# Forming the second phase's weights beside the phase change instead of two blocks earlier

## The chip, the cores and the metric

The kernel runs on one core of one Trainium2 chip. The metric is the device time of one launch in microseconds (us); lower is better. A core has a matrix engine (TensorE, PE in the profile; its weight loads are listed as PEld), a vector engine (DVE), a scalar engine (ACT), GpSimd (POOL) and the sync engine (SP). Each runs its own queue of instructions in order. Transfers between device memory (DRAM) and on-chip memory (SBUF) are issued here by the SP, ACT and POOL queues; matrix products go to eight banks of PSUM, from which DVE or ACT must move them ("evict").

## The reference, cut to what matters

With one layer only the pooling mixer runs. x is 4096 x 1024, the model width 1024.

```python
normed = rms_norm(h, norm_w[i])
u, gate = jnp.split(h @ in_w, 2, axis=-1)        # in_w: 1024 x 2048, h is normed here
pooled = trailing means of u over 2, 4, 8, 16 rows (one window per 256 columns) - u
mixed  = einsum(pooled, group_w) + group_b       # per group of 256 columns
y = mixed * scale * silu(gate)
out = rms_norm(x + y @ out_w, final_norm_w)
```

All is float32.

## The kernel before, in words

**Folding and transposing.** The group map commutes with the pooling over rows, so the kernel folds `group_w` into the first half of `in_w` once, at the start (`fold`, L284). It keeps activations transposed, channels on the 128 partitions, and so works on 512 x 512 quarters of each 1024 x 1024 product.

**Products.** Each 1024 x 1024 x 1024 block product is made of seven half-size products P1 to P7 (a Strassen-Winograd scheme) instead of eight. For both operands this needs sums and differences of quarters: with quarters 11, 12, 21 and 22 of the weights, `combine` (L219) forms S = 22 - 12 for P7, T = 11 + S for P6, 22 - T for P5 and 21 - T for P4; P1, P2 and P3 use 11, 21 and 22 as they are. Order in the kernel: P1, P2, P6, P7, P5, P4, P3 (`ORDER_IN`).

**Splits.** For float32 accuracy each operand is split in two: a rounded high part (an ACT copy, L151) and the rest (a DVE subtraction, L145). `split` (L153) does both; `split_scaled` (L215) also multiplies rows by a column of scales. TensorE then runs three matmuls per tile, high x high, high x low, low x high (`mm3`, L457, L460). One product of the first two phases is 48 matmuls of 128x512.

**Phases and steps.** `steps` (L774) lists the work. Phase "a" makes columns 0 to 511 of both halves of the input projection (value path and gate), phase "b" columns 512 to 1023, each for four blocks of 1024 rows: 4 x 7 products a phase. Phase "o", the output projection with residual and final norm, has eight blocks of 512 rows with seven products of half the length. The loop at L995 runs step n: it loads ahead (three steps, L976), forms combinations, splits the operand of the next step, runs the product and evicts it (`run`, L808). The seven weight operands of a phase lie in `w[P1]` to `w[P7]`, in two tiles each (halves of the contraction, h = 0 and 1), and stay for all four blocks.

**Row statistics.** The first norm's row factors of the next block are computed during the current one: squares on ACT (L320), five small DVE instructions (`stats`, `rsqrt`), a 2 KB store to `rd` (L336) and a load that spreads it over all partitions (L363). `normalize` (L365, DVE at L148) multiplies the x tiles by it. The first half's factors are stored at step P5, the second's at P3; the second's are used by `normalize_a2` (L434) at P1 of the next block, from which S and T of the activations, and the splits, follow.

**Weights of phase b.** In blocks 1 and 2 of phase a, after product P5, `make_wb(h)` (L239) loads two pieces of `in_w` (L199) and two of the folded weights `wvd` (L243, L244), scales rows on ACT (L213), stores 11 and 21 to DRAM scratch `wbd` (L233, L234), combines on DVE (L142, L145) and stores the other five (L236). In the last block of phase a, right after product Pi has run, `load_w` (L257) loads both tiles of `wbd[i]` (L260) and splits them into `w[i]`, whose old content is no longer needed. Phase o's weights go the same way one phase later (`make_wo`, `wod`).

**Buffers and order.** Tiles come from two pools of 4 KB a partition, `st` (11) and `vt` (8), taken and given back in turn (`Slots`); a transfer into a tile waits for all that used it before. A scheduler places the instructions of each engine's queue from program order and priorities; `tc.issue_after(x)` keeps what is recorded under it behind x. Four tiles `ops` hold split activation operands; a step uses two.

Of the kernel before, what the change touches and what calls it, by code (L numbers as in the profile page):

```python
# [10 lines left out]
F32 = mybir.dt.float32  # L11
F32R = mybir.dt.float32r
AF = mybir.ActivationFunctionType
ALU = mybir.AluOpType

P = 128
D = 1024
S = 4096
H = 512
TB = 1024  # L20
NB = S // TB
# [9 lines left out]
P1, P2, P3, P4, P5, P6, P7 = range(1, 8)  # L31
ORDER_IN = (P1, P2, P6, P7, P5, P4, P3)
# [28 lines left out]
def kernel(  # L61
# [32 lines left out]
    nc = tc.nc  # L94
# [5 lines left out]
    dram = ctx.enter_context(tc.tile_pool(name="dram", bufs=1, space=bass.MemoryType.DRAM))  # L100
# [3 lines left out]
    def new_w(i):  # L104
        return [
            mem.tile([P, 2, 2, H], F32R, tag=f"w{i}_{h}", name=f"w{i}_{h}") for h in range(2)
        ]

    w = {i: new_w(i) for i in (P1, P2, P6, P7)}
# [18 lines left out]
    def take(pattern="p (a b) -> p a b", pool=None, **sizes):  # L128
        sizes = sizes or {"a": 2}
        if pool is None:  # L130
            spare = len(vt.free) > keep[0] or not st.free
            pool = vt if spare and vt.age() < st.age() else st
        return pool.take(lambda t: t[:, 0:D].rearrange(pattern, **sizes))
# [4 lines left out]
    def give(ap):  # L138
        next(p for p in (st, vt, early, early5) if id(ap) in p.used).give(ap)
# [4 lines left out]
    def sub(dst, a, b):  # L144
        nc.vector.tensor_tensor(out=dst, in0=a, in1=b, op=ALU.subtract)  # L145
# [4 lines left out]
    def copy(dst, src, func=AF.Copy):  # L150
        return nc.scalar.activation(dst, src, func)  # L151

    def split(dst, src):  # L153

        copy(dst[:, 0], src)
        sub(dst[:, 1], src, dst[:, 0].bitcast(F32))

    colt = const.tile([P, 24], F32, name="colt")
    norm_c = [colt[:, k : k + 1] for k in range(NK)]
    bias_c = [colt[:, 8 + k : 9 + k] for k in range(NK)]  # L160
# [2 lines left out]
    tails = const.tile([P, 2, 2, HIST], F32, name="tails")  # L163

    wvd = [dram.tile([P, 2, H], F32, name=f"wvd{k}") for k in range(4)]
    wbd = {
        i: [dram.tile([P, 2, H], F32, name=f"wbd{i}_{h}") for h in range(2)]
        for i in range(P1, P7 + 1)
    }
    wod = {  # L170
        i: [dram.tile([P, 2, H], F32, name=f"wod{i}_{h}") for h in range(2)]
        for i in range(P1, P7 + 1)
# [24 lines left out]
    def load_rows(mat, k, c):  # L197
        u = take()
        nc.sync.dma_start(  # L199
            out=u, in_=mat[k * P : (k + 2) * P, c : c + H].rearrange("(t p) c -> p t c", p=P)  # L200
        )
        return u
# [8 lines left out]
    def scale_rows(u, cs):  # L211
        for j in range(2):
            nc.scalar.activation(u[:, j], u[:, j], AF.Copy, scale=cs[j])  # L213

    def split_scaled(dst, u, cs):  # L215
        for j in range(2):
            copy_scaled(dst[:, :, j], u[:, j], cs[j])
# [10 lines left out]
    def pair(cs, h, kh):  # L228
        k = 4 * kh + 2 * h
        return cs[k : k + 2]  # L230

    def store_weights(dst, h, b11, b21, b12, b22):
        nc.sync.dma_start(out=dst[P1][h], in_=b11)  # L233
        nc.sync.dma_start(out=dst[P2][h], in_=b21)  # L234
        for i, u in combine(b11, b21, b12, b22).items():
            nc.sync.dma_start(out=dst[i][h], in_=u)  # L236
            give(u)

    def make_wb(h):  # L239
        g0 = load_rows(in_w, 2 * h, D + H)  # L240
        g1 = load_rows(in_w, 4 + 2 * h, D + H)
        v0, v1 = take(), take()
        nc.sync.dma_start(out=v0, in_=wvd[h])  # L243
        nc.sync.dma_start(out=v1, in_=wvd[2 + h])  # L244
        scale_rows(g0, pair(norm_c, h, 0))
        scale_rows(g1, pair(norm_c, h, 1))
        store_weights(wbd, h, g0, g1, v0, v1)

    def make_wo(h):
        us = {}  # L250
        for n in range(2):
            for kh in range(2):
                us[kh, n] = load_rows(out_w, 4 * kh + 2 * h, n * H)
                scale_rows(us[kh, n], pair(scale_c, h, kh))
        store_weights(wod, h, us[0, 0], us[1, 0], us[0, 1], us[1, 1])

    def load_w(src, i):  # L257
        for h in range(2):
            u = take()
            nc.sync.dma_start(out=u, in_=src[i][h])  # L260
            split(w[i][h], u)
            give(u)
# [296 lines left out]
    ev, evicted = {}, [None]  # L559
# [248 lines left out]
    def run(n, between=None):  # L808
        kind, b, i = steps[n]
        sets = sets_of(kind, b)  # L810
        if kind == "o":
            product_out(i, split_up.pop(n), sets, n == len(steps) - 1)
            evict_o(b, i, sets)
        else:
            product_in(i, split_up.pop(n), sets, i == P1, between)
            evict_in(b, 0 if kind == "a" else 1, i, sets)
# [30 lines left out]
    gw, ru, g0 = [None] * 2, {}, []  # L847
# [14 lines left out]
    v0, v1 = [None] * 2, [None] * 2  # L862
# [23 lines left out]
    g1 = [load_rows(in_w, 4 + 2 * h, D) for h in range(2)]  # L886
# [108 lines left out]
    for n in range(2, len(steps)):  # L995
        kind, b, i = steps[n]
        ahead = kind == "a" and b + 1 < NB
        keep[0] = 5 if kind == "b" and b == NB - 1 else 3
        advance("load", n, load, load_reach)
        if ahead:  # L1000
            rows, squares = row_plan(b)
            for half, rs in scales.items():
                store_rs(b + 1, half, rs)
                load_rstd(b + 1, half)
            scales.clear()
            for j in squares.get(i, ()):
                with tc.issue_after(evicted[0]):
                    square_row(b + 1, j // 4, j % 4)
                if j % 4 == 3:
                    scales[j // 4] = stats(b + 1, j // 4)  # L1010
            for j in rows.get(i, ()):
                load_row(b + 1, j // 4, j % 4, early if b == 0 and i == P6 else None)
        if kind == "a" and b > 0 and i == P1:
            normalize_a2(b)
        if n > 2:
            form(n + 2)
        advance("split", n, split_step, split_reach)
        if n == 2:
            form_s4(0)
            form(n + 2)  # L1020
        if kind == "a" and b == 0:
            rest_of_first(n)
        pool_due(n)
        run(n)
        if kind in ("a", "b"):
            pool_later(n)
            if kind == "a":
                pool_due(n)
            if b == NB - 1:
                load_w(wbd if kind == "a" else wod, i)  # L1030
            if i == P5:
                if kind == "a" and b in (1, 2):
                    make_wb(b - 1)
                elif kind == "b" and b in (1, 2):
                    make_wo(b - 1)
            if kind == "b" and b == NB - 1 and i == P3:
                f = take("p (a b) -> p a b", a=2)
                nc.sync.dma_start(
                    out=f.rearrange("p a b -> p (a b)"), in_=final_w.partition_broadcast(P)
                )  # L1040
                fw.append(f)
# [52 lines left out]
```

## Time and profile before

| what | us |
|---|---|
| median of three runs (971.11 to 971.44) | 971.4 |
| the profiled execution | 973.14 |
| its span, first to last instruction | 971.0 |
| PE busy | 951.5 |
| DVE busy | 745.6 |
| ACT busy | 452.2 |
| first product step of phase a starts | 39.74 |
| phase b starts | 353.62 |
| phase o starts | 658.26 |
| last product step starts | 957.46 |
| mean granted TensorE clock | 0.997 of full |

A row of busy times by stretch reads: stretch, its length, then busy us (and instructions) of PE, PEld, DVE, ACT and POOL, the granted clock, the DMA engines' busy share and GB/s. A row of the chain of waits reads: start, length, what the kernel's end hung on in that time; "DMA a<-b" is the time of a transfer. A row of DMA issues reads: tiles, issuing queue, count, size, median us from issue to landing.

### The profile page before, as it was taken

The numbers are of one execution on the slowest core, as the hardware profiler recorded it, in microseconds if no ns is written. First come the engines' busy times: TensorE is split into PE (matmuls) and PEld (weight loads), VectorE is DVE, ScalarE is ACT, GpSimd is POOL, SyncE is SP. The second block draws the span as 40 slices with busy tenths as digits, with TensorE's granted clock in tenths as the row PEclk, the third lists the DMA queues.
The fourth block names the chain that finished last, engine by engine and source line by source line (L and its number), as shares of the span: only waits on it lengthen the run. The fifth ranks groups of instructions, "written<-read, shape, count | busy, mean of one in ns | idle before, by whom it ended". The sixth has DMA issues, their size and how long they took to land.

```text
span 971.0 us, 11079 instructions
## 1 busy us (share of the span) xinstructions
PE 951.5 (98%) x4190; PEld 786.4 (81%) x4190; DVE 745.6 (77%) x907; ACT 452.2 (47%) x679; POOL 6.7 (1%) x16
## 2 busy tenths in 40 slices
PE   8899999989999999999999999999999999999996
PEld 7778888878877888888888888888888888888885
DVE  5696993886899794497598499599978677677675
ACT  4759438337545554345444435553424324324233
POOL 0100000000000000000000000000000000000000
PEclk9999999999999999999999999999999999999998
DMA  9964865977977624115714714646646446356022
GB/s 340 411 271 141 265 246 186 339 274 220 333 251 245 210 93 146 44 44 182 273 44 158 267 75 147 222 151 195 225 155 227 131 151 217 111 194 216 22 87 87
DMA packets 68933, 184.35 MB, mean 190 GB/s; under 512 B 6928, under 2 KB 24464, under 8 KB 68880
## 3 DMA queue, kind: packets, MB, share of 16 engines
q1 hardware_dynamic: 62976, 163.71, 49.1%
q10 hardware_dynamic: 4176, 13.65, 3.5%
q0 software_dynamic: 1728, 6.29, 1.6%
q8 instruction: 33, 0.54, 0.2%
q14 instruction: 20, 0.16, 0.1%
HBM read 116.50 MB, written 67.12 MB: 189 GB/s over the span
## 4 chain that ended last, share of the span: by engine, by line
PE 75%; DMA 10%; DVE 8%; ACT 4%; issue 1%; SPq 0%; ACTq 0%; DVEq 0%
PE bank L460 73%; DMA st<-in_in_w 3%; DMA rd<-rs 2%; DMA st<-rd 2%; DVE op L145 2%; PE bank L289 1%; DMA wbd<-vt 1%; DVE vt L142 1%; ACT vt L320 1%; DVE st L145 1%; DVE st L148 1%; DMA wbd<-st 1%; DMA early<-in_wut 1%; DVE st L546 1%; DVE vt L148 1%
## 5 line engine op out<-in xcount | busy, mean ns | idle before, releaser
L460 PE MATMUL bank<-op,w 128*128 128x512 f32 x2688 | 612.0, 389 | 5.6 <-DVE op L145 4.7
L460 PEld LDWEIGHTS bank<-op,w 128*128 128x128 f32 x2688 | 504.1, 188 | 112.7 <-DVE op L145 7.0
L460 PE MATMUL bank<-w,op 128*128 128x512 f32 (+1 forms) x1356 | 305.0, 387 | 0.0
L460 PEld LDWEIGHTS bank<-w,op 128*128 128x128 f32 x1356 | 253.1, 188 | 51.9
L151 ACT ACTIVATE op<-st 128x1024 fp32r<-128x1024 f32 x121 | 127.7, 1057 | 148.6 <-PE bank L460 108.2
L145 DVE TENSOR_TENSOR op<-st,op 128x1024 fp32r<-128x1024 f32 x121 | 147.3, 1223 | 58.9 <-ACT op L151 58.7
L142 DVE TENSOR_TENSOR vt<-vt 128x1028 f32<-128x1028 f32 (+6 forms) x72 | 88.0, 1235 | 1.7 <-DMA wbd<-vt 1.6
L151 ACT ACTIVATE op<-vt 128x1024 fp32r<-128x1024 f32 x45 | 47.4, 1059 | 81.1 <-PE bank L460 68.6
L142 DVE TENSOR_TENSOR st<-bank,st 128x512 f32<-128x512 f32 x76 | 52.0, 689 | 36.4 <-PE bank L460 34.3
L151 ACT ACTIVATE vt<-bank 128x512 f32<-128x512 f32 x94 | 54.8, 594 | 35.8 <-PE bank L460 34.2
L142 DVE TENSOR_TENSOR vt<-bank,vt 128x512 f32<-128x512 f32 (+1 forms) x85 | 56.7, 679 | 15.1 <-PE bank L460 8.7
L145 DVE TENSOR_TENSOR op<-vt,op 128x1024 fp32r<-128x1024 f32 x45 | 54.9, 1223 | 14.7 <-ACT op L151 14.6
L145 DVE TENSOR_TENSOR w<-st,w 128x1024 fp32r<-128x1024 f32 x32 | 39.1, 1224 | 21.4 <-ACT w L151 21.2
L151 ACT ACTIVATE w<-st 128x1024 fp32r<-128x1024 f32 x32 | 33.7, 1060 | 38.0 <-PE bank L460 28.7
L151 ACT ACTIVATE bank<-bank 128x512 f32<-128x512 f32 x48 | 27.9, 582 | 46.3 <-PE bank L460 29.9
L145 DVE TENSOR_TENSOR st<-st,st 128x1024 f32<-128x1024 f32 x38 | 46.2, 1224 | 2.4 <-DMA st<-wvd 1.9
L148 DVE TENSOR_TENSOR st<-st,st 128x1024 f32<-128x1024 f32 (+1 forms) x22 | 25.4, 1175 | 26.5 <-DMA st<-rd 18.3
L151 ACT ACTIVATE st<-bank 128x512 f32<-128x512 f32 x36 | 20.5, 594 | 20.0 <-DMA yd<-st 10.8
L541 DVE SCALAR_TENSOR_TENSOR vt<-vt,vt 128x1024 f32<-128x1024 f32 x24 | 29.4, 1226 | 0.1
L289 PE MATMUL bank<-early,early 128*128 128x256 f32 x128 | 28.3, 380 | 1.1 <-DVE st L297 1.1
L289 PEld LDWEIGHTS bank<-early,early 128*128 128x128 f32 x128 | 24.2, 190 | 4.7 <-DVE st L297 1.5
L142 DVE TENSOR_TENSOR st<-st,st 128x1024 f32<-128x1024 f32 x21 | 25.4, 1226 | 0.1
(109 smaller groups left out, 415.8 us busy)
## 6 DMA issues: line engine op xcount, KB each, us to landing
st<-in_x SPq DMA_DIRECT2D x32, 512.0 KB, 4.5
st<-sd SPq DMA_DIRECT2D x29, 512.0 KB, 4.5
vt<-in_x SPq DMA_DIRECT2D x27, 512.0 KB, 4.9
st<-in_xt SPq DMA_DIRECT2D x20, 512.0 KB, 5.9
st<-yd SPq DMA_DIRECT2D x19, 512.0 KB, 4.1
yd<-st SPq DMA_DIRECT2D x17, 512.0 KB, 3.5
out<-st SPq DMA_DIRECT2D x17, 512.0 KB, 5.1
sd<-st ACTq DMA_DIRECT2D x16, 512.0 KB, 5.6
```

The lines of the kernel that those rows point to most:

```text
L142: nc.vector.tensor_tensor(out=dst, in0=a, in1=b, op=ALU.add)
L145: nc.vector.tensor_tensor(out=dst, in0=a, in1=b, op=ALU.subtract)
L148: nc.vector.tensor_tensor(out=dst, in0=a, in1=b, op=ALU.mult)
L151: return nc.scalar.activation(dst, src, func)
L289: nc.tensor.matmul(ps2[kk][:, j * 256 : (j + 1) * 256], r[:, kk, 2 * j + t, :], g[:, 2 * j + t, :], start=(t == 0), stop=(t == 1),)
L320: nc.scalar.activation(u[:, 0], u[:, 0], AF.Square, accum_out=sums[b, half][:, j : j + 1])
L460: nc.tensor.matmul(ps, a, b, start=start and n == 0, stop=stop and n == 2, skip_group_check=True)
L541: nc.vector.scalar_tensor_tensor(out=s[:, :, at : at + H], in0=s[:, :, at : at + H], scalar=1.0 / win, in1=v[:, :, HIST:], op0=ALU.mult, o ...
L546: nc.vector.scalar_tensor_tensor(out=sg[:, j], in0=s[:, j, at : at + H], scalar=bias_c[2 * grp + j], in1=sg[:, j], op0=ALU.add, op1=ALU.mult,)
```

## The change

The scratch `wbd` goes, and with it the early `make_wb` and, for phase b's weights, `load_w`. The new `load_wb(i)` loads the sources that product i's weights are made of: pieces of `in_w`, of `wvd`, or both. The new `make_wb(i)` forms the weights from them directly. P1 and P2 are scaled and split in one go; P6, P7, P5 and P4 form their sums on DVE, with the row scaling inside the same instruction (`scaled`); P5 forms the negative of its operand and splits it with a sign (`split_negative`); the tile T of P6 is kept in `t2` until P4. Several sources are therefore loaded more than once.

The loop calls `make_wb` two steps after the product has run, from the third step of phase a's last block (P6) to the second step of phase b, under `tc.issue_after` of the last recorded ACT eviction, and loads the sources of the next one right behind it. Phase o's weights are made as before.

```diff
--- before.py
+++ after.py
@@ -155,6 +155,13 @@
         copy(dst[:, 0], src)
         sub(dst[:, 1], src, dst[:, 0].bitcast(F32))
 
+    def split_negative(dst, src):
+        nc.scalar.activation(dst[:, 0], src, AF.Copy, scale=-1.0)
+        nc.vector.scalar_tensor_tensor(
+            out=dst[:, 1], in0=src, scalar=-1.0, in1=dst[:, 0].bitcast(F32),
+            op0=ALU.mult, op1=ALU.subtract,
+        )
+
     colt = const.tile([P, 24], F32, name="colt")
     norm_c = [colt[:, k : k + 1] for k in range(NK)]
     bias_c = [colt[:, 8 + k : 9 + k] for k in range(NK)]
@@ -163,10 +170,6 @@
     tails = const.tile([P, 2, 2, HIST], F32, name="tails")
 
     wvd = [dram.tile([P, 2, H], F32, name=f"wvd{k}") for k in range(4)]
-    wbd = {
-        i: [dram.tile([P, 2, H], F32, name=f"wbd{i}_{h}") for h in range(2)]
-        for i in range(P1, P7 + 1)
-    }
     wod = {
         i: [dram.tile([P, 2, H], F32, name=f"wod{i}_{h}") for h in range(2)]
         for i in range(P1, P7 + 1)
@@ -236,15 +239,57 @@
             nc.sync.dma_start(out=dst[i][h], in_=u)
             give(u)
 
-    def make_wb(h):
-        g0 = load_rows(in_w, 2 * h, D + H)
-        g1 = load_rows(in_w, 4 + 2 * h, D + H)
-        v0, v1 = take(), take()
-        nc.sync.dma_start(out=v0, in_=wvd[h])
-        nc.sync.dma_start(out=v1, in_=wvd[2 + h])
-        scale_rows(g0, pair(norm_c, h, 0))
-        scale_rows(g1, pair(norm_c, h, 1))
-        store_weights(wbd, h, g0, g1, v0, v1)
+
+
+    parts, t2 = {}, {}
+
+    def load_wb(i):
+        for h in range(2):
+            p = parts[i, h] = {}
+            if i in (P1, P6, P5):
+                p["11"] = load_rows(in_w, 2 * h, D + H)
+            if i in (P2, P4):
+                p["21"] = load_rows(in_w, 4 + 2 * h, D + H)
+            for name, k, used in (("12", h, (P6, P7, P5)), ("22", 2 + h, (P6, P7, P3))):
+                if i in used:
+                    p[name] = take()
+                    nc.sync.dma_start(out=p[name], in_=wvd[k])
+
+    def scaled(u, cs, other, op):
+
+        for j in range(2):
+            nc.vector.scalar_tensor_tensor(
+                out=u[:, j], in0=u[:, j], scalar=cs[j], in1=other[:, j], op0=ALU.mult, op1=op
+            )
+
+    def make_wb(i):
+
+        for h in range(2):
+            p = parts.pop((i, h))
+            top, bottom = pair(norm_c, h, 0), pair(norm_c, h, 1)
+            if i == P1:
+                split_scaled(w[i][h], p["11"], top)
+            elif i == P2:
+                split_scaled(w[i][h], p["21"], bottom)
+            elif i == P6:
+                sub(p["12"], p["22"], p["12"])
+                scaled(p["11"], top, p["12"], ALU.add)
+                t2[h] = p.pop("11")
+                split(w[i][h], t2[h])
+            elif i == P7:
+                sub(p["22"], p["22"], p["12"])
+                split(w[i][h], p["22"])
+            elif i == P5:
+                scaled(p["11"], top, p["12"], ALU.subtract)
+                split_negative(w[i][h], p["11"])
+            elif i == P4:
+                scaled(p["21"], bottom, t2[h], ALU.subtract)
+                split(w[i][h], p["21"])
+                give(t2.pop(h))
+            else:
+                split(w[i][h], p["22"])
+            for u in p.values():
+                give(u)
 
     def make_wo(h):
         us = {}
@@ -1022,17 +1067,20 @@
             rest_of_first(n)
         pool_due(n)
         run(n)
+        since = n - (NB - 1) * len(ORDER_IN) - 2
+        if 0 <= since < len(ORDER_IN):
+            with tc.issue_after(evicted[0]):
+                make_wb(ORDER_IN[since])
+        if 0 <= since + 1 < len(ORDER_IN):
+            load_wb(ORDER_IN[since + 1])
         if kind in ("a", "b"):
             pool_later(n)
             if kind == "a":
                 pool_due(n)
-            if b == NB - 1:
-                load_w(wbd if kind == "a" else wod, i)
-            if i == P5:
-                if kind == "a" and b in (1, 2):
-                    make_wb(b - 1)
-                elif kind == "b" and b in (1, 2):
-                    make_wo(b - 1)
+            if kind == "b" and b == NB - 1:
+                load_w(wod, i)
+            if kind == "b" and b in (1, 2) and i == P5:
+                make_wo(b - 1)
             if kind == "b" and b == NB - 1 and i == P3:
                 f = take("p (a b) -> p a b", a=2)
                 nc.sync.dma_start(
```

## The prediction, made before the changed kernel was run

> **What bounds the kernel now.** I read the page's busy shares first, then the busy time of each engine in stretches cut at the starts of the product steps, then the chain of waits, then the DMA issues.
>
> ```profile
> PE 951.5 (98%) x4190; PEld 786.4 (81%) x4190; DVE 745.6 (77%) x907; ACT 452.2 (47%) x679; POOL 6.7 (1%) x16
> ...
> 183.72:194.60 10.88, 10.88 (x50) 9.01 (x48) 9.28 (x13) 3.82 (x4) 0.00 (x0) 1.00 0.95 334
> 194.60:207.66 13.06, 11.17 (x50) 8.93 (x48) 9.96 (x10) 4.72 (x10) 0.00 (x0) 1.00 0.91 305
> 207.66:219.83 12.17, 11.21 (x49) 8.93 (x48) 12.17 (x13) 4.55 (x6) 0.00 (x0) 1.00 0.65 237
> ...
> 285.11:298.35 13.24, 11.18 (x49) 8.93 (x48) 13.24 (x15) 6.33 (x10) 0.00 (x0) 1.00 0.49 181
> 298.35:310.11 11.76, 11.20 (x50) 8.94 (x49) 11.76 (x11) 8.00 (x13) 0.00 (x0) 1.00 0.75 256
> ...
> 310.11:957.46 647.35, 647.35 (x2857) 536.21 (x2856) 493.02 (x587) 269.04 (x385) 0.00 (x0) 1.00 0.44 152
> ```
>
> TensorE (PE) is the bound: from 310.11 us to the end of the last product step it never stops, at full granted clock. An undisturbed step of the first or second phase lasts 10.88 us. I call a step by phase, block and product: a2P1 is product P1 of block 2 in the first phase, b0P1 opens the second. Only four steps after 140 us are longer: a2P1 13.06, a2P2 12.17, a3P2 13.24, a3P6 11.76. Their excess is 2.18 + 1.29 + 2.36 + 0.88 = 6.71 us, and since PE is solid behind them, each us saved there reaches the end.
>
> ```profile
> core 0 of [0], span 971.0 us
> ...
> 253.47 7.17 DMA wbd<-vt
> ...
> 263.19 9.02 DMA rd<-rs
> 272.21 0.02 issue
> 272.23 4.95 DMA st<-rd
> 277.17 0.02 issue
> 277.20 1.23 DVE st L148
> ...
> 299.30 320.82 PE bank L460 x1414
> ```
>
> The chain shows why they are late: DVE waits for a store of `wbd` before a tile is free; the row statistics are stored late (9.02 us), read back (4.95 us), and only then normalised (L148). At the boundary before it the same chain has 6.54 us for the store and 7.09 for the load.
>
> ```profile
> st<-wbd SPq DMA_DIRECT2D x14, 512.0 KB, 4.3
> ...
> st<-in_in_w SPq DMA_DIRECT2D x6, 512.0 KB, 6.2
> ...
> st<-wvd SPq DMA_DIRECT2D x3, 512.0 KB, 4.9
> ...
> rd<-rs SPq DMA_DIRECT2D x6, 2.0 KB, 4.3
> ```
>
> These are median times from issue to landing; I use them below.
>
> **The change, part by part.** (1) Traffic. Gone: 14 stores and 14 loads of `wbd` and 8 source loads; new: 22 source loads. That is 14 half-MB transfers fewer. It costs nothing by itself; what counts is where they wait.
>
> (2) Blocks 1 and 2 lose the old make_wb: on DVE 8 combinations of 128x1024. Started back to back in this profile, such an instruction takes 1.135 us of the queue (1.22 busy), so 9.1 us; on ACT 8 scalings of 0.67 us; on the SP queue 22 DMAs. In the SP queue the row statistics stood behind wbd stores, and on DVE the five small steps that make them stood between combinations that waited for `wvd`. In the changed build's queues they stand directly behind the split for the product P3 (and behind some x loads).
>
> For a2 I walk DVE by durations of rows. Its first normalisation comes at 165.85 as before; up to the statistics of the other half the new queue holds 9 instructions of 128x1024 at 1.135, 4 evictions from PSUM at 0.60, six small ones at 0.1 and a wait of 0.6 for an x load, 13.8 us: ready at 179.7 (184.6 before). The same store-and-load took 8.4 us for the other half, where nothing delayed it (157.46 to 165.83; 8.3 at 237.77). From the first normalisation to the split for a2P2 the new queue holds 10 x 1.135 + 4 x 0.66 (128x512 from SBUF) + 0.60 (PSUM eviction) = 14.6 us. 179.7 + 8.4 + 14.6 = 202.7; due one step after a2P1's start, at 205.5: 2.8 to spare. For a3, with a2 on time, the first normalisation moves from 246.05 to 242.6; 10 x 1.135 + 4 x 0.60 + 0.6 later, at 256.9, the statistics are ready; + 8.4 + 15.2 (one eviction more) = 280.5, due eight steps after a2P1's start, at 281.6: 1.1 to spare. So all 6.71 us come back. Bounds: the loaded chain took 14.1 us (263.15 to 277.20), and with it, 5.7 more, 2.9 us would be lost at a2P2 and 4.6 at a3P2. I take 8.4, as the neighbouring stores that crowded the 14.1 are the ones removed.
>
> (3) The weights are now formed in a3P6 to b0P2. DVE did 14 splits there (15.9 us). It now does 8 scaled splits of 128x512 at 0.66, 12 scaled sums of 128x512 at 0.66, 4 differences and 10 splits at 1.135: 5.3 + 7.9 + 4.5 + 11.4 = 29.1, 13.2 us more. ACT has 8 x 0.67 + 10 x 1.06 instead of 14 x 1.06; it is half idle and hidden. The weights themselves are in no hurry: w for P6, for example, is ready some 40 us before b0P6. What counts is the operand splits behind them on DVE.
>
> From the split for a3P2 to that for b0P6 the new DVE queue holds 46 instructions at 1.135, 32 at 0.66 and 8 evictions at 0.60: 52.2 + 21.1 + 4.8 = 78.1 us. Between the two due times lie 8 steps, 87.0 us, plus the 1.1 to spare: 88.1. So DVE may idle 10.0 us. It will idle three times at the head of the queue for a `wvd` load: the differences for P6 (half 0), P7 (half 0) and P6 (half 1). In each case the tile to be filled comes free just before, SP issues the load then, and only one instruction of 1.135 stands between. With a landing time L each costs L - 1.1; a fourth wait (P4's rows) costs about 0.5. Behind the waiting difference stand the splits for a3P5, a3P4 and later ones; PE waits for these, but they have 5 us or more to spare, so the lag is first due at b0P1 and most at b0P6.
> L is 4.3 by the wbd loads of this stretch, 4.9 by the wvd loads of earlier, busier blocks. I take 4.6: 3 x 3.5 + 0.5 = 11.0, loss 1.0 us. With 3.2, about the shortest half-MB load here, the loss is 0; with 6.2 (the loads of in_w) it is 15.8 - 10.0 = 5.8.
> The Trainium skill ("DMA: Bandwidth & Descriptors", section Anatomy of one DMA) gives a DMA 2.0 us fixed plus its bytes at 436 GB/s, by which I estimate 3.2 us for 512 KB; the fastest loads here agree, the medians do not, and by the page the loss would be 0 and the time 964.7.
>
> (4) SP's queue in this stretch: a source load whose tile is not yet free holds up the loads of b0's operands behind it. b0P1's second half is issued some 35 us before its split, its first half behind the P2 split, some 25 us before. Covered, unless a landing takes over 20 us.
>
> (5) From b0P7 on DVE catches up (b0P7 and b0P5 each had 2.45 us of DVE work in 10.88), and spares of 9 to 14 us follow. Cost 0; if that cover were gone, b0P7's split would be next, with about 1 us.
>
> **Sum.** Profiled execution 973.14 us (span 971.0, 2.1 around it): -6.7 + 0.0 + 1.0 = -5.7, so 967.4 for it; it stands 1.7 above the median of 971.4, from which the same sum gives 965.7.
>
> **Rivals.** A difference within 0.2% (1.9 us) cannot be told from none.
>
> B, the boundaries stay late. The row statistics still share the DMA engines with eight half-MB stores of the operands (ACT's queue) and the x loads. For it: 6.5 and 9.0 us for a 2 KB store at a DMA share of 0.7 to 0.9. Against: 2.9 and 4.5 for the other half, and wbd's stores gone. At 14.1 us for a2 alone: 971.4 - 6.7 + 2.9 + 1.0 = 968.6; for a3 alone, with its spare gone: 971.4 - 6.7 + 4.6 + 2.1 = 971.4. The Trainium skill (same page, section Issuing engines are not separate DMA queues) says that DMAs of all issuers run on the same 16 engines and interleave, so moving work between queues frees nothing; the 9.02 us store bears this out.
>
> C, slower: DVE's three waits at the phase change. If the wvd loads land as the longest of this profile (7.5 us), DVE idles 3 x 6.4 + 0.5 = 19.7, 9.7 over its spare: 971.4 - 6.7 + 9.7 = 974.4. It makes the kernel slower from L = 7.2. For it: several loads are issued within 2 us there, and landings of 5.5 to 6.6 us occur in such a cluster around 310 us. Against: each of these loads is issued only when DVE moves on, so they hold themselves apart.
>
> D, nothing changes: the four late steps come from normalising, not from make_wb, and stay. For it: a1P1 and a1P2, with no make_wb before them, lose 0.17 and 0.49 us. Against: that is a tenth. 971.4.
>
> **How the numbers follow.** Forecast (964.7 to 968.5) 0.70; B 0.13; C 0.11; D 0.06. Faster: 0.70 and half of B, 0.77. Same: D and the other half, 0.12. Slower: C, 0.11. The range 964.5 to 971.0 holds the forecast and nearly all of B, and leaves out C and D; the likeliest case's own range is 964.7 to 968.5, or L from 3.2 to 5.6.
>
> **What would show it.** Right: a2P1 to a3P6 at 10.88 us each; the store of statistics issued near 180 and 257 us; no wbd; DVE waits on wvd of about 3 us each in a3P6 to a3P4; b0P6 at most some us long and no other step of the second phase. Wrong: a2P2 or a3P2 still over 12 us (B), or b0P1 to b0P6 together 10 us long (C), or a step of a later block that waits.

## The result and the profile after

The changed kernel took 968.66 us (median of six runs, 965.78 to 969.10), against 971.42 us before (968.91 to 972.55): a ratio of 0.9968, 95% interval 0.9955 to 0.9982. Two later series on other chips gave 0.9973 (0.9959 to 0.9988; 968.10 against 970.83 us) and 0.9970 (0.9959 to 0.9981; 966.98 against 969.66). So it is faster by 2.7 to 2.8 us, where the sum forecast 5.7. Of the ten executions of `a_double22` below, one took 1379.77 us at a granted clock of 0.654; it is left out of that run's numbers.

The profiled execution of the changed kernel took 965.78 us (span 964.0): 7.36 us less than that of the kernel before at 973.14. The first lies at the lower end of its kernel's times and the second at the upper end of its own, and this matters below. First the page's busy shares, then the stretches of the four steps that were late and of the one that the prediction feared (us from and to, length, PE busy, PEld, DVE, ACT, POOL, granted clock, DMA share, GB/s); the stretches are a2P1, a2P2, a3P2, a3P6, b0P6 and all that follows.

```profile
PE 950.8 (99%) x4190; PEld 787.3 (82%) x4190; DVE 749.5 (78%) x919; ACT 449.5 (47%) x675; POOL 6.7 (1%) x16
```

```profile
194.35:205.22 10.87, 10.87 (x49) 9.01 (x48) 10.87 (x11) 5.46 (x10) 0.00 (x0) 1.00 0.81 302
205.22:216.10 10.88, 10.88 (x49) 9.01 (x48) 10.88 (x12) 4.15 (x6) 0.00 (x0) 1.00 0.84 264
281.38:292.26 10.88, 10.88 (x49) 9.01 (x48) 10.88 (x11) 4.52 (x7) 0.00 (x0) 1.00 0.48 171
292.26:303.14 10.88, 10.88 (x49) 9.01 (x48) 5.50 (x6) 4.63 (x7) 0.00 (x0) 1.00 0.67 234
368.43:379.39 10.96, 10.96 (x49) 8.93 (x48) 10.96 (x13) 6.31 (x8) 0.00 (x0) 1.00 0.70 245
379.39:950.59 571.20, 571.20 (x2521) 473.13 (x2520) 439.35 (x532) 231.50 (x336) 0.00 (x0) 1.00 0.44 152
```

The four late steps last 10.87 to 10.88 us, all 6.71 us are back, and PE does not stop behind them. The statistics' stores, DMA `rd<-rs`, are issued at 178.35 and 254.39 us and are back in 8.2 and 6.7 us, store and load together. b0P6 is 0.08 us longer than an undisturbed step. What DVE waited for from 290 to 380 us shows the price of that stretch (us in total, times, longest):

```profile
DVE st L145 <- DMA st<-wvd: 11.0, 3, 4.6
DVE op L145 <- ACT op L151: 1.3, 1, 1.3
DVE st L261 <- DMA st<-in_in_w: 0.8, 1, 0.8
```

Three waits for `wvd`, 11.0 us in all, and 0.8 for P4's rows; the prediction said 3 x 3.5 + 0.5. The landing times on the page (median, last column) are 4.6 us for `wvd`, as taken, and 3.6 for the 2 KB store, where it was 4.3.

```profile
st<-wvd SPq DMA_DIRECT2D x12, 512.0 KB, 4.6
...
rd<-rs SPq DMA_DIRECT2D x6, 2.0 KB, 3.6
```

Two questions were left. What made the four steps late: the stores of make_wb, its combinations, or neither? And why is the gain, median against median, 2.8 us and not 5.7?

### The profile page after: what moved, and what is told of

Its sections match the earlier page's. It is cut to its first block, busy times and chain, and to the rows that moved or that the text cites. A ratio compares the mean times of both kernels' runs of the same rounds, so it can differ in the third digit from the quotient of the medians.

```text
span 964.0 us, 11053 instructions
## 1 busy us (share of the span) xinstructions
PE 950.8 (99%) x4190; PEld 787.3 (82%) x4190; DVE 749.5 (78%) x919; ACT 449.5 (47%) x675; POOL 6.7 (1%) x16
## 4 chain that ended last, share of the span: by engine, by line
PE 98%; DVE 1%; ACT 0%; issue 0%
PE bank L505 95%; PE bank L334 3%; PE bank L885 1%; DVE w L145 0%; PE bank L396 0%; DVE st L937 0%; DVE early L145 0%; ACT w L151 0%; DVE vt L783 0%; DVE st L783 0%; DVE st L342 0%; DVE w L389 0%; ACT st L749 0%; DVE op L883 0%; DVE vt L142 0%
## 5 line engine op out<-in xcount | busy, mean ns | idle before, releaser
L151 ACT ACTIVATE op<-st 128x1024 fp32r<-128x1024 f32 x115 | 121.4, 1056 | 151.5 <-PE bank L505 117.8
L145 DVE TENSOR_TENSOR op<-st,op 128x1024 fp32r<-128x1024 f32 x115 | 139.7, 1218 | 50.8 <-ACT op L151 50.4
L151 ACT ACTIVATE op<-vt 128x1024 fp32r<-128x1024 f32 x51 | 53.8, 1058 | 84.0 <-PE bank L505 70.6
L142 DVE TENSOR_TENSOR vt<-vt 128x1024 f32<-128x1024 f32 (+6 forms) x72 | 87.7, 1227 | 0.1
L145 DVE TENSOR_TENSOR op<-vt,op 128x1024 fp32r<-128x1024 f32 x51 | 62.1, 1219 | 13.3 <-ACT op L151 13.3
L151 ACT ACTIVATE vt<-bank 128x512 f32<-128x512 f32 x88 | 51.5, 596 | 43.2 <-PE bank L505 34.6
L142 DVE TENSOR_TENSOR vt<-bank,vt 128x512 f32<-128x512 f32 (+1 forms) x83 | 55.2, 677 | 15.0 <-PE bank L505 10.8
L145 DVE TENSOR_TENSOR st<-st,st 128x1024 f32<-128x1024 f32 x36 | 43.5, 1218 | 11.6 <-DMA st<-wvd 11.0
L151 ACT ACTIVATE bank<-bank 128x512 f32<-128x512 f32 x48 | 27.9, 582 | 34.9 <-PE bank L505 30.5
L145 DVE TENSOR_TENSOR w<-st,w 128x1024 fp32r<-128x1024 f32 x23 | 27.7, 1219 | 12.6 <-ACT w L151 12.4
L151 ACT ACTIVATE w<-st 128x1024 fp32r<-128x1024 f32 x23 | 24.1, 1059 | 25.1 <-PE bank L505 15.4
L151 ACT ACTIVATE st<-bank 128x512 f32<-128x512 f32 x42 | 24.6, 596 | 23.3 <-PE bank L505 15.4
L591 DVE SCALAR_TENSOR_TENSOR st<-vt,colt,st 128x512 f32<-128x512 f32 x40 | 28.4, 743 | 0.0
```

The costliest lines, as they stand in the source:

```text
L142: nc.vector.tensor_tensor(out=dst, in0=a, in1=b, op=ALU.add)
L591: nc.vector.scalar_tensor_tensor(out=sg[:, j], in0=s[:, j, at : at + H], scalar=bias_c[2 * grp + j], in1=sg[:, j], op0=ALU.add, op1=ALU.mult,)
```

## The experiments

### What made the four steps late

The first two runs take the early make_wb out of the kernel before, in whole or only its stores.

`b_no_make` (where no source is given, the split's tile is loaded from `wvd`):

```diff
-                load_w(wbd if kind == "a" else wod, i)
+                load_w(None if kind == "a" else wod, i)
...
-                if kind == "a" and b in (1, 2):
-                    make_wb(b - 1)
```

> The kernel before without its early make_wb: none of its source loads, scalings, combinations or wbd stores; the seven weight splits of the second phase take the raw wvd tiles where they took wbd tiles, at the same places and with as many 512 KB loads. Left out is the forming of the second phase's weights, so its products are of other weights. My account (make_wb alone makes the four late steps): a2P1, a2P2, a3P2 and a3P6 last 10.88 us, the statistics' store is issued near 180 and 257 us, time 971.4 - 6.7 = 964.7 us. Rival B (statistics late by the operand stores and x loads that stay): a2P2 or a3P2 still over 12 us, 967.6 to 969.3. Rival D (the late steps come from normalising): 971.4.

Measured: 965.91 us (965.69 to 966.65) against 970.83 us for the kernel before on that chip, ratio 0.9954 (0.9940 to 0.9967). All the four steps last 10.88 us, and between 130 and 400 us PE waits for nothing. Rivals B and D fall: the operand stores and x loads are all still there, and so is the normalising, and no boundary is late. But the gain on the medians is 4.9 us, not 6.7.

`b_no_store` keeps the loads, scalings and combinations:

```diff
-        store_weights(wbd, h, g0, g1, v0, v1)
+        for u in combine(g0, g1, v0, v1).values():
+            give(u)
```

> The kernel before with make_wb's loads, scalings and combinations as they are, but none of the 14 wbd stores: the combined tiles are given back at once, and the later splits take raw wvd tiles. Left out is the storing of the formed weights, so the second phase works with other weights. If what makes the steps late is the wait for the wbd stores (tiles that come free late, and the statistics' store behind 512 KB stores in SP's queue), most of the 6.71 us goes: 964.7 to 966.5 us. If it is the eight combinations of 1.135 us in DVE's queue and their wait for wvd, the four late steps stay within 1 us of what they were: 970 to 971.4.

Measured: 965.92 us (965.26 to 966.45), ratio 0.9952 (0.9938 to 0.9966), the same as without any make_wb. The stretches of a2P1 and a3P2 in its profile:

```profile
193.96:204.84 10.88, 10.88 (x50) 9.01 (x48) 10.88 (x11) 4.59 (x8) 0.00 (x0) 1.00 0.92 375
281.00:291.88 10.88, 10.88 (x50) 9.01 (x48) 10.88 (x13) 7.38 (x11) 0.00 (x0) 1.00 0.50 175
```

With the eight combinations a block still in DVE's queue both steps are whole. In this profile a statistics' store still takes 6.5 us (issued at 181.40), and it costs nothing, since it is issued 10.7 us earlier than in the kernel before (192.11).

`b_no_combine` is the complement: the 14 stores stay and the combinations go.

```diff
-        store_weights(wbd, h, g0, g1, v0, v1)
+        for i, u in ((P1, g0), (P2, g1), (P6, g0), (P7, v0), (P5, v1), (P4, g1), (P3, v1)):
+            nc.sync.dma_start(out=wbd[i][h], in_=u)
+        for u in (g0, v0, g1, v1):
+            give(u)
```

> The kernel before with make_wb's loads, scalings and 14 wbd stores, but without the eight combinations on DVE: the scaled rows and the raw wvd tiles are stored instead. Left out is the combining, so the second phase works with other weights. If the stores make the steps late, they stay: 970 to 971.4 us. If DVE's combinations do (9.1 us of its queue a block and their wait for wvd), most of the 6.71 us goes: 964.7 to 966.5. If each alone takes more time than the steps have to spare, this run and the one without stores both stay above 967.

Measured: 972.68 us (969.64 to 974.22), ratio 1.0018 (1.0008 to 1.0029). Lines of its chain of waits from 250 to 300 us (start, us, what), and the stretch of a3P2:

```profile
251.36 8.35 DMA wbd<-vt
...
261.05 9.62 DMA rd<-rs
270.68 0.02 issue
270.69 3.60 DMA st<-rd
274.29 0.02 issue
274.31 1.23 DVE st L148
```

```profile
282.15:298.22 16.07, 13.21 (x50) 9.60 (x48) 16.07 (x17) 7.65 (x12) 0.00 (x0) 0.89 0.53 196
```

It is the chain of the kernel before again: a wait for `wbd`, a 2 KB store of 9.62 us, the load, then the normalising. Here the whole lateness falls on a3P2, 5.19 us, of which PE waited only 2.9; its granted clock is 0.89 in that step (more on this in the last section). So at the boundary to a3 the stores alone make the steps late. At the boundary to a2 they do not: in this profile a2P1 and a2P2 last 10.88 us, as they do without the stores, so it takes stores and combinations together to lose the 3.47 us there. The combinations by themselves make no step late.

What the `wbd` stores did at a3 can be followed on SP's queue in the kernel before (start, us, transfer and count):

```profile
257.34 4.80 SPq L393 DMA_DIRECT2D st<-in_xt  x2
262.19 0.90 SPq L393 DMA_DIRECT2D vt<-in_xt  x2
263.19 1.48 SPq L336 DMA_DIRECT2D rd<-rs  x1
```

The second load of x waited 3.2 us for a `wbd` store that still held its tile. So three 512 KB loads of x went out from 261.81 to 262.71 us, right ahead of the statistics' store. No `wbd` store was in flight during the 9.02 us of that store; it landed 0.6 us after the last of these loads. In `b_no_combine` the loads of x waited 5.4 us for `wbd` stores, and five went out in the 3.6 us ahead of the store of 9.62 us. In the changed kernel the last three go out within 2.7 us from 242.75 us on, and the store at 254.39 lands in 3.7 us.

One of the four late steps was not held by an operand. In a2P2 of the kernel before, PE stood still for 0.96 us for a bank that ACT had not evicted:

```profile
208.22 2.60 ACTq L384 DMA_DIRECT2D sd<-vt  x2
210.86 0.58 ACT L151 ACTIVATE bank<-bank 128x512 f32<-128x512 f32 x1 [7.86 <-DMA sd<-vt]
211.50 74.00 PE L460 MATMUL bank<-op,w 128*128 128x512 f32 x325 [0.96 <-ACT bank L151]
```

ACT's queue held the stores of two operand tiles, which wait for the late normalising on DVE, and the eviction stood behind them.

### Why the gain is smaller on the medians

`a_again` is the changed kernel, unedited; `b_again` is the kernel before, unedited.

> The changed kernel once more, as it is. Its six times lay at two levels, 965.8 to 966.4 and 968.6 to 969.1 us. Theory 1 (the phase change): at the upper level one of the three waits for wvd lasts some 3 us longer and b0P6, whose operand was 0.13 us late in the profile at the lower level, or a step behind it is longer by 2.5 to 3 us. Theory 2 (the start): the steps from a1P1 on last what they did, and a1P1 begins 2.5 to 3 us later than at 118.2. Theory 3 (B): a2P1 to a3P6 hold the difference.

Measured: 968.10 us (966.12 to 971.16), a profile at 968.88. The stretch of b0P6 in it, and DVE's waits from 290 to 380 us:

```profile
369.40:382.47 13.07, 11.18 (x50) 8.93 (x48) 13.07 (x14) 7.18 (x11) 0.00 (x0) 1.00 0.68 226
```

```profile
DVE st L145 <- DMA st<-wvd: 12.9, 3, 4.8
DVE st L261 <- DMA st<-in_in_w: 0.7, 1, 0.7
```

b0P6 is 2.19 us too long, against 0.08 in the profile at 965.78. Another 0.85 us lies ahead of a1P1 (119.02 against 118.17) and 0.1 in a1P2: 2.1 + 0.85 + 0.1 is the 3.1 us between the two profiles. Theory 1 holds for two thirds of the difference and theory 2 for most of the rest; theory 3 falls.

> The kernel before, again. Its profile at 973.14 us stands above its median (971.4, 970.9), and the kernel without the early make_wb gained 4.9 us on the median instead of the 6.71 of that profile. If the late steps vary from run to run, this profile shows the same four steps (a2P1, a2P2, a3P2, a3P6) late by another sum, 4 to 6 us at a time of 970 to 971.5. If they are late by 6.7 again, the difference of the two levels lies at the start, ahead of a1P1.

Measured: 970.70 us (967.87 to 973.09), ratio to the kernel before 1.0007 (0.9994 to 1.0020), a profile at 969.93. The four late steps in it:

```profile
194.70:207.24 12.54, 11.22 (x50) 8.93 (x48) 9.88 (x11) 4.15 (x9) 0.00 (x0) 1.00 0.89 303
207.24:218.90 11.66, 11.19 (x50) 8.93 (x48) 11.66 (x13) 4.72 (x6) 0.00 (x0) 1.00 0.67 245
284.20:295.55 11.35, 11.17 (x49) 8.93 (x48) 11.35 (x13) 5.06 (x9) 0.00 (x0) 1.00 0.51 193
295.55:307.30 11.75, 11.18 (x50) 8.93 (x48) 11.75 (x11) 7.64 (x12) 0.00 (x0) 1.00 0.75 255
```

Their excess over 10.88 is 1.66 + 0.78 + 0.47 + 0.87 = 3.78 us, where the profile at 973.14 has 6.71. Of the 3.21 us between these two executions 2.93 lie in these four steps. The expectation named 4 to 6 us, so even that was too much; that the late steps vary from run to run is shown.

### The account of DVE at the phase change

For every profile, DVE's work and waits from the end of the split for a3P2 to the end of the split for b0P6 (of the first half of each operand) can be set against eight steps (87.04 us) and the time to spare at a3P2. What is over is the loss that the prediction's step (3) speaks of. The figures are summed from the trace's DVE instructions.

| profile | spare at a3P2 | work | idle | loss by the sum | b0P1 to b0P6 too long by |
|---|---|---|---|---|---|
| prediction | 1.1 | 78.1 | 11.0 | 1.0 | - |
| changed, 965.78 | 4.90 | 78.9 | 13.15 | 0.1 | 0.08 |
| changed (`a_again`), 968.88 | 3.14 | 78.9 | 13.6 | 2.2 | 2.19 |
| changed (`a_again2`), 967.10 | 4.90 | 79.0 | 13.7 | 0.7 | 0.67 |
| `a_keep_s2` | 2.76 | 79.0 | 10.45 | none | 0.00 |
| `a_double22` | 3.48 | 77.7 | 16.55 | 3.7 | 5.29 |

The sum gives the loss to within 0.05 us in the changed kernel. It is bookkeeping, since work and idle time add up to the time that passed: that it comes out shows that there PE was held by this split alone, and not what made the idle time. The next runs press on its terms.

`a_keep_s` and `a_keep_s2` (one kernel, on two chips) keep the difference of the two `wvd` tiles:

```diff
-            for name, k, used in (("12", h, (P6, P7, P5)), ("22", 2 + h, (P6, P7, P3))):
+            for name, k, used in (("12", h, (P6, P5)), ("22", 2 + h, (P6, P3))):
...
+                s2[h] = p.pop("12")
             elif i == P7:
-                sub(p["22"], p["22"], p["12"])
-                split(w[i][h], p["22"])
+                split(w[i][h], s2[h])
+                give(s2.pop(h))
```

> The changed kernel, but the difference of the two wvd tiles that P6 needs is kept and used again for P7's weight: four 512 KB loads and two differences of 1.135 us fewer, and one of the three waits for wvd (3.2 to 3.5 us in the two profiles) gone. If the loss at b0P6 (0.1 and 2.2 us in the two profiles of the changed kernel) is DVE's lag, b0P6 gets 3 to 5 us to spare, lasts 10.88 us, and the time is that of the kernel without the early make_wb, 965.9 us, within 0.7, with a smaller spread than the 966.1 to 971.2 of the changed kernel. If the upper level comes from elsewhere (the start, the granted clock), the time stays at 968.1 with the same spread, and only b0P6's slack changes. If the wait only moves on to the next difference (P6, half 1), b0P6 gains 2.3 us or less.

Measured: 966.44 us (965.94 to 969.49), ratio 0.9956 (0.9940 to 0.9972). b0P6 lasts 10.88 us, but has only 0.27 us to spare, not 3 to 5. Much of the work and waits saved was filled at once by work that the queue now held earlier: DVE's work in the stretch is not 2.3 us smaller but 0.1 to 0.4 larger.

> The kernel with the difference of the wvd tiles kept, again, to set it beside the changed kernel on one chip. If its gain is the loss at b0P6 (0.1 to 2.2 us) it is some 1.5 us faster than the changed kernel: 966.4 against 968.1 us, and the intervals of the two ratios lie apart or nearly so. If the 966.4 was chance of a chip, both come out within 0.5 us.

Measured beside the changed kernel on one chip: 966.24 us (965.28 to 967.04), ratio 0.9960 (0.9948 to 0.9972).

> The changed kernel again: 968.1 us within 0.7, at a ratio to the kernel before of 0.997. In its profile b0P6 is between 10.9 and 13.5 us long by the same account, and no other step of the first two phases behind a1P2 is longer than 10.9.

Measured: 966.98 us (966.20 to 968.12), ratio 0.9970 (0.9959 to 0.9981). The time is 0.4 us below what was expected, the ratio as expected; b0P6 is 11.55 us long and no other step behind a1P2 is longer than 10.9. The two intervals overlap, so 0.7 us in favour of the kept difference is likely and not settled; the 1.5 expected did not come, and in its profile the changed kernel lost only 0.67 us at b0P6. The stretch of b0P6 in `a_keep_s2`, and DVE's waits from 290 to 371 us:

```profile
358.71:369.59 10.88, 10.88 (x50) 9.01 (x48) 10.88 (x13) 5.96 (x8) 0.00 (x0) 1.00 0.52 189
```

```profile
DVE st L145 <- DMA st<-wvd: 7.8, 2, 4.9
DVE vt L261 <- DMA st<-wvd: 1.4, 1, 1.4
DVE op L145 <- ACT op L151: 1.3, 1, 1.3
```

One wait of the three is gone and a shorter one has come.

`a_double22` goes the other way:

```diff
                     nc.sync.dma_start(out=p[name], in_=wvd[k])
+                    if i in (P6, P7) and name == "22":
+                        nc.sync.dma_start(out=p[name], in_=wvd[k])
```

> The changed kernel with the second wvd load of P6 and of P7 issued twice into the same tile, the second behind the landing of the first, so that each of the three differences on DVE waits one landing longer: by the profile 3.2 to 4.6 us each, 10 to 13 us in all. By my account each us of these waits goes to b0P6 once the slack there is used up (it is): b0P1 to b0P6 together 10 to 13 us longer, most of it in b0P6 or b0P1, and the time 968.1 + 10 to 13 = 978 to 981. If DVE still has time to spare there, or if the waits end by something other than the loads, the loss is much smaller: 968 to 972.

Measured: 970.34 us (median of nine, 965.71 to 972.34), ratio 0.9992 (0.9975 to 1.0008). The 978 to 981 us of the account failed by 7.7 us or more; the time lies in the 968 to 972 of the other case. DVE's waits from 290 to 330 us, and the stretch of b0P6:

```profile
DVE st L145 <- DMA st<-wvd: 12.8, 3, 4.9
DVE op L145 <- ACT op L151: 3.7, 1, 3.7
```

```profile
370.24:385.45 15.21, 12.80 (x49) 10.10 (x48) 15.21 (x15) 8.21 (x11) 0.00 (x0) 0.89 0.65 215
```

The three waits did not become one landing longer each. The last difference ran 6 to 8 us later than in the two first profiles of the changed kernel, counted from a3P6's start, but only about half of that was waiting; the rest was work that DVE's queue now held ahead of the waits. DVE idled 16.55 us instead of 13.15 to 13.7. The sum of the table gives a loss of 3.7 us; 5.29 were lost, and the granted clock of 0.89 accounts for the rest (last section). So of the 10 to 13 us that the account added to the waits, some 3 became idle time of DVE: the changed program is scheduled anew, and work that had stood behind the waits now stood ahead of them.

`a_work8` puts work instead of waits behind the third wait: the DVE half of P5's split five times over.

```diff
                 split_negative(w[i][h], p["11"])
+                for _ in range(4):
+                    nc.vector.scalar_tensor_tensor(
+                        out=w[i][h][:, 1], in0=p["11"], scalar=-1.0,
+                        in1=w[i][h][:, 0].bitcast(F32), op0=ALU.mult, op1=ALU.subtract,
+                    )
```

> The changed kernel with the DVE half of P5's weight split done five times over instead of once, for both halves: eight more instructions of 128x1024 at 1.135 us, 9.1 us of DVE's queue, behind all three waits for wvd and ahead of the operand splits of b0P2 and b0P6. If the loss is DVE's lag as my account sums it (no slack left at b0P6), all 9.1 us reach the end: b0P2 and b0P6 together 9 to 10 us longer than in the changed kernel, time 968.1 + 9.1 = 977.2 us, within 1.5. If DVE had slack to absorb it (the rival that the late step has another cause), 968 to 972.

Measured: 979.44 us (976.39 to 982.57), ratio 1.0097 (1.0070 to 1.0123). The median is 0.7 us above the expected 977.2 within 1.5. The four runs fall into two pairs, at 976.4 and 982.5; the profile is of the lower pair, within the expectation, and why the upper pair took 6 us more was not seen. In the profile:

```profile
357.42:376.08 18.66, 12.53 (x49) 9.92 (x48) 18.66 (x20) 5.79 (x7) 0.00 (x0) 0.82 0.17 56
376.08:389.99 13.91, 11.72 (x49) 8.93 (x48) 13.41 (x13) 7.39 (x10) 0.00 (x0) 1.00 0.56 190
```

b0P2 and b0P6 are 7.78 + 3.03 = 10.8 us too long, 8.6 to 10.7 more than in the changed kernel. In this execution eight instructions of 1.135 us, 9.1 us, came through whole: DVE has nothing to spare there.

### The order behind the evictions

`a_no_after` takes away the one thing that holds the weight splits behind the evictions of the product that has just run:

```diff
-            with tc.issue_after(evicted[0]):
-                make_wb(ORDER_IN[since])
+            make_wb(ORDER_IN[since])
```

> The changed kernel without the order that puts the weight splits behind the evictions of the product that has just run: they go into DVE's queue as early as the program names them, ahead of evictions and of operand splits. Theory 1: what counts is the sum of DVE's work and waits up to b0P6, which is the same (46 instructions at 1.135, 32 at 0.66, the same loads): 968.1 within 1.5 us. Theory 2: the waits for loads now stand ahead of evictions or of splits that have less to spare (a3P6 6.5 and 4.8 us), and a step of a3 or b0P1 is late by some us more: 970 to 975. Theory 3: the waits overlap better with what DVE has to do, and b0P6 has some us to spare: 965.9.

Measured: 968.85 us (967.99 to 972.65), ratio 0.9988 (0.9975 to 1.0002). By the time it is theory 1, by the place it is none of the three. The stretch of b0P2, and what ACT waited for from 340 to 372 us:

```profile
358.36:371.60 13.24, 11.47 (x50) 8.86 (x48) 13.24 (x14) 8.03 (x10) 0.00 (x0) 1.00 0.51 183
```

```profile
ACT w L151 <- DVE st L261: 6.9, 1, 6.9
```

b0P6 now has 4.4 us to spare, but b0P2 is 2.36 us too long, and not for an operand (the first half was split 9.9 us ahead of the step, the second 2.0). ACT's queue held a weight copy that waited 6.9 us for a DVE sum, and behind it an eviction; PE waited for that bank. In these profiles the order behind the evictions thus guards ACT's evictions, and the lag falls on b0P6; without it the loss is of the same size elsewhere.

### A small lag, and the clock

`a_work2` is `a_work8` with one repetition for each half instead of four (`range(1)` for `range(4)`): 2.3 us of DVE.

> The changed kernel with the DVE half of P5's weight split done twice instead of once, for both halves: two more instructions of 128x1024, 2.3 us of DVE's queue, behind the waits for wvd and ahead of the operand splits of b0P2 and b0P6. PE then stands still at b0P6 for about 2.3 us more than in the changed kernel (0.1, 0.7 and 2.2 us in three profiles), some 2.4 to 4.5 us. If the loss is this lag alone: b0P6 13.3 to 15.4 us long, granted clock 1.00 behind it, time 967.0 to 968.1 + 2.3 = 969.3 to 970.4. If a standstill of 2.1 us or more also halves the granted clock for some 3 us, as it did in the kernels with doubled loads (2.41 us, then matmuls at 427 instead of 227 ns) and without combinations (2.14 us): eight matmuls at 0.2 us more, 1.6 us on top, b0P6 or the step behind it 15 to 17 us, time 971 to 972.

Measured: 971.56 us (968.15 to 972.83), ratio 1.0001 (0.9989 to 1.0014), the profile at 971.20. PE from 340 us on, and the stretches of b0P2 up to the end of the standstill, just behind it, and from there to b0P6:

```profile
339.74 22.60 PE L510 MATMUL bank<-op,w 128*128 128x512 f32 x99
364.25 8.90 PE L510 MATMUL bank<-op,w 128*128 128x512 f32 x31 [1.90 <-ACT bank L151]
373.88 18.43 PE L510 MATMUL bank<-op,w 128*128 128x512 f32 x80 [0.73 <-DVE op L145]
```

```profile
358.10:364.25 6.15, 4.25 (x20) 3.19 (x18) 6.15 (x6) 1.60 (x3) 0.00 (x0) 1.00 0.51 171
364.25:368.00 3.75, 3.75 (x10) 2.93 (x11) 3.75 (x5) 1.59 (x2) 0.00 (x0) 0.54 0.00 0
368.00:372.75 4.75, 4.75 (x22) 3.94 (x21) 4.75 (x7) 3.85 (x6) 0.00 (x0) 1.00 0.27 110
```

The time is that of the second theory, by a path that neither named. ACT waited 6.4 us for a DVE combination (`ACT op L151 <- DVE st L145`) with an eviction behind it, so PE stood still for 1.90 us in the middle of b0P2, and then ran for 3.75 us at a granted clock of 0.54. b0P2 is 3.77 us too long and b0P6 1.03, 4.8 together: 2.6 to 4.7 more than in the changed kernel, for 2.3 us of DVE work.

## Why the prediction was right, and where its sum was not

*The number.* The medians of the three series are 968.66, 968.10 and 966.98 us. The first lies just above the forecast's own range (964.7 to 968.5) and only within the wide one, which reached to 971.0 to hold rival B. B did not come, so that this median still fell within the range was luck.

*Part (1), traffic.* 177.0 MB instead of 184.4. That this is worth nothing by itself was not shown, since no run takes away the traffic alone. What the runs without stores and without combinations show is what the 14 stores of the early make_wb held up.

*Part (2), the boundaries.* Right in place, and right that the early make_wb made the steps late. One reason was wrong: the 14.1 us of store and load were to fall to 8.4 "as the neighbouring stores that crowded the 14.1 are the ones removed". The neighbours were loads of x that had waited for tiles held by `wbd` stores; that they moved away with the stores came out right without having been foreseen. Statistics ready at 179.7 and 256.9 us were forecast, 178.35 and 254.39 came; the 8.4 us for store and load became 8.2 and 6.7; the spare of 2.8 us at a2P2 was 3.9, that of 1.1 at a3P2 between 3.1 and 4.9. For a3 the mis-sized term is the 8.3 us of the first half's store and load, which took 6.6 us once the `wbd` stores were gone; the second half's took 6.7 instead of 8.4.

*The size of part (2)* is the term of the sum that failed. 6.71 us was read from one profile at 973.14 us, and the prediction took its distance of 1.7 us to the median as something around the sum ("from which the same sum gives 965.7"). The distance lay in the very steps that were to be won: at 969.93 us they lose 3.78. Taken away on one chip, they gave 4.9 us on the medians. Had the 1.7 been put where it belonged, the sum would have been 6.7 - 1.7 - 1.0 = 4.0 us and 967.4.

*Part (3), the phase change.* A loss of 1.0 us was forecast; 0.08, 2.19 and 0.67 us were measured, and the place, b0P6, is as named. That the mean is so close was luck, as the terms were off and made up for each other: spare 2 to 4 us larger, work 0.8 larger, idle 2.2 to 2.7 larger, by a wait for ACT (1.3 us) or a longer wait at the first difference (4.8 us). Its price per us of L, three times L, was too steep: with the doubled loads the idle time grew by some 3 us where the doubling should have added 10 to 13. Rival C had the same slope, so the L of 7.2 us from which it would decide is too low. In the Trainium skill ("DMA: Bandwidth & Descriptors", section Anatomy of one DMA) the formula that this part takes is a fit for transfers that GpSimd issues. The `wvd` loads are issued by SP, and landed in 4.6 us where it gives 3.2.

*Part (3), ACT "half idle and hidden"* holds for the changed kernel alone. In two neighbours of it (`a_no_after`, `a_work2`), and at a2P2 of the kernel before, ACT's queue carried DVE's lag on to the evictions, and PE waited for a bank.

*Parts (4) and (5)* held: no step from b0P7 on is longer, though b0P7 had only 1.8 us to spare, and no operand load of b0 was waited for.

*The rivals.* B and D are refuted by the runs without make_wb and without stores. The 9.02 us store that B rested on was crowded by loads of x, as B said. But they stood there because of the `wbd` stores: with the combinations gone and those stores kept the store takes 9.62 us. In `b_no_store` one still takes 6.5 us behind four loads of x, and makes no step late.

*What is open.* On the median the changed kernel gained 2.7 to 2.8 us, where 4.9 less about 1.0 would make 3.9. Some of the rest lies ahead of a1P1, which begins at 118.06 to 119.02 us in the profiles of the changed kernel and its variants, and at 117.78 and 117.90 in the two of the kernel before. In eight of those nine profiles (all but `a_keep_s`) the granted clock is halved for 3.41 us from some 28 to 30 us on, and the first product step begins at 40.57 to 41.05 us; in `a_keep_s`, in the two of the kernel before, in `b_no_make` and in `b_no_store` it is not, and that step begins at 39.53 to 39.74. This is likely a part of the missing 1.1 us, but `b_no_combine` has it too, and why it comes with one program and not with the other was not tested. No profile fell on its slowest runs (970.9 to 971.2 us), so what they lose is not known.

## What to carry to other kernels

A sum made from one profile inherits the luck of that execution: where its time is off the median, look first whether the difference lies in the very waits that the change removes, and scale the gain by a second profile. A lag on one in-order engine reaches the bound engine by every queue that waits on it; here it came by operands and by another engine's evictions. A removed DMA is worth what it held up: here 14 stores of half a megabyte cost 4.9 us on the median, in part because loads that waited for their tiles then went out right ahead of a 2 KB store on which a boundary hung.

## What the runs showed of the hardware

A standstill of PE can cost nearly twice its length. Behind four of them matmuls started 427 ns apart instead of 227: behind 2.41 us in `a_double22`, 2.14 in `b_no_combine`, 1.90 in `a_work2` and 6.13 in `a_work8`. Eight matmuls at 0.2 us more cost 1.6 us, which explains the difference between the two last columns of the table for `a_double22`, 1.59 us. But 1.89 and 2.06 us of standstill in the kernel before and 1.90 us in `a_again` left the clock at 1.00.

The place of the standstill decides as well as its length. In all 14 profiles the times at which the granted clock changes lie whole multiples of 3.413 us apart: it was halved for 3.41 us in the first three cases above and for 6.83 in `a_work8`, and in the changed kernel it was full for 928.42 us, 272 times 3.413. If the profiles are cut into stretches at such times, PE was idle for 1.90 us or more in every one of the 27 stretches in which full clock last held before a halved one (14 of them at the kernel's end), and for 1.87 us or less in every stretch ahead of one at full clock. Two neighbouring stretches of `a_again` and two of `a_work2` lie on either side of that limit:

```profile
369.88:373.30 3.42, 1.62 (x7) 1.36 (x8) 3.42 (x4) 1.94 (x4) 0.00 (x0) 1.00 0.64 208
373.30:376.71 3.41, 3.41 (x17) 2.83 (x16) 3.41 (x4) 1.35 (x2) 0.00 (x0) 1.00 0.40 156
```

```profile
361.11:364.53 3.42, 1.52 (x7) 0.98 (x6) 3.42 (x4) 1.88 (x3) 0.00 (x0) 1.00 0.44 156
364.53:367.94 3.41, 3.41 (x9) 2.64 (x9) 3.41 (x5) 1.25 (x2) 0.00 (x0) 0.50 0.00 0
```

The 1.90 us of `a_work2` fall into one stretch; of those of `a_again` 0.1 us belong to the stretch before, so 1.80 are left; the 2.06 us of the kernel before are divided into 1.31 and 0.75. The Trainium skill ("TensorE: Matmul & The Clock Gate", section Part 1: The HAM clock gate) says that the array's clock is halved after an idle window of about 3.4 us, and that this window runs on freely without regard to the kernel. The half clock, the length of the window and its free run agree with these profiles; that the window has to be idle throughout, if it is read so, does not, as 1.90 us of 3.41 were enough, and here the measurement decides.

A 2 KB store to memory took 1.7 us with nothing beside it (`b_no_store`, issued at 256.84 us, DMA share 0.04), 6.5 us in the same profile behind four 512 KB loads that SP had issued in the 3.7 us before, and 9.0 and 9.6 us in the kernel before and in `b_no_combine` behind four and five such loads. In the last three cases it landed 0.2 to 0.6 us after the last of these loads.
